# Where the high and low products of a row stand, and an even recurrence that is solved transposed, in a tuned four-layer trunk on one core

## The chip, the core and the metric

The kernel runs on one NeuronCore of a Trainium2 chip. Five engines run their own instruction streams and meet at semaphores: TensorE (PE, with its weight loads listed as PEld), VectorE (DVE), ScalarE (ACT), GpSimd (POOL) and SyncE (SP), which here issues all the DMAs. The metric is the device time of one execution in microseconds (us); lower is better.

## What is computed

Two layers over 256 tokens of width 2048 (fp32). Layer 0 is "even": one input projection feeds an RWKV-7 mixer (group A, 16 heads of 64) and an RG-LRU (group B), then one output projection. Layer 1 is "odd": sparse attention. Both are followed by a gated FFN of width 5632 and by a sigmoid-gated projection of p ("PLE").

```python
def reference(x, p, ...):
    for layer in range(DEPTH):
        j = layer // 2
        if layer % 2 == 0:
            z = x @ ev_w_in[j]
            y_a = rwkv7_mix(z[..., :A_COLS], ...)
            y_b = rglru_mix(z[..., A_COLS:], ...)
            y = jnp.concatenate([y_a, y_b], axis=-1) @ ev_w_out[j]
        else:
            y = dsa_mix(x, ...) @ od_w_out[j]
        x = layer_norm(DN_ALPHA * x + y, ln1_g[layer], ln1_b[layer])
        x = layer_norm(DN_ALPHA * x + conv_ffn(x, ffn_w_up[layer], ...), ln2_g[layer], ln2_b[layer])
        x = x + jax.nn.sigmoid(x @ ple_w_gate[layer]) * (p[layer] @ ple_w_proj[layer])

def rwkv7_mix(z, ...):
    ...
    def step(state, inp):
        r_t, w_t, k_t, v_t, kk_t, a_t = inp
        sa = jnp.einsum('bhvk,bhk->bhv', state, -kk_t)
        state = state * w_t[:, :, None, :] + sa[..., None] * (kk_t * a_t)[:, :, None, :] + v_t[..., None] * k_t[:, :, None, :]
        return state, jnp.einsum('bhvk,bhk->bhv', state, r_t)
    ...
    ym = jnp.mean(y, -1, keepdims=True)
    yv = jnp.mean(jnp.square(y - ym), -1, keepdims=True)
    y = ((y - ym) * lax.rsqrt(yv + A_GN_EPS)).reshape(bsz, seq, A_WIDTH) * gn_g + gn_b
    bonus = (jnp.sum(r * k * r_k, -1, keepdims=True) * v).reshape(bsz, seq, A_WIDTH)
    return ((y + bonus) * g).astype(z.dtype)
```

## The kernel before

Channels lie on partitions, the 256 tokens in the free dimension. Every large weight is read once, in chunks of 128x1024 (512 KB): `wchunk` (L143) has SP load it into `raw` (three buffers), ACT makes the rounded high half `hi`, DVE the rest `lo = raw - hi` (five buffers each). Activations x are split the same way, so that a product needs three parts: hi by x-high and x-low, lo by x-high.

**Rows of products.** In `mm3` (L164) a weight block of 128x128 is used in two matmuls, "H" (hi, 512 columns: both halves of x) and "L" (lo, 256 columns), or, with `one`, in three of 256 columns (L171 to L173). A row (one tile of 128 outputs) has 16 blocks, 44 in the FFN's down projection. The 88 rows of FFN up from row 3 on go through `ordered` (L178), in an order that `row_order(j)` (L41) gives: three rows of four are plain, H then L for each block (L then H in one group of five), and the last of four has in its second half a turn from HL to LH or back, eight H and then eight L ("8/8"), two H and then two L ("2/2", blocks 12 and 13), or one H split in two, each once in 20 rows. FFN down, the PLE gate, odout and evout are plain H, L.

**Even layer.** The 16 heads of A are done in 8 pairs i (128 channels, 4 chunks of 64 tokens). `stage1(i)` makes the pair's r, k, v from the input projection (`block`, three rows of 16 blocks with `one`) and the factors of the chunked recurrence (AR, be, ka, ...). `stage2(i)` solves the recurrence, as a chain that hops between PE, DVE and ACT: be by AR, whose diagonal 16x16 blocks are packed in `Y16`; X, which spreads Y16 over 128x512 twice; two matmuls of X by the constant `ones16` (L863) and two ACT copies, which put it as `B` on all partitions; 15 steps on DVE that invert the small blocks (`M`); their spread `Dt`; E by Dt (FT), Dt by RHS (Z1), three times FT by Z (`four`, L829: four fp32 matmuls of 128x128); gb by R1; then the four chunks in turn (L935 `ub` by R1, L936 `vb` by R2, L938 the state), and `cen` by y (L954), which takes the mean off y. fp32 products count two matmul records each in the trace. While a hop of stage2 is under way PE works on filler: `stage2` yields what it needs (table `W`, in us of filler), and `run` takes that from `filler(i)`: `stage1(i+1)`, then by `FILL` the RG-LRU block i (`rglru`, two rows of 16 blocks and two matmuls by `bw`); in the last pair rows of evout as well. Fillers use the `pp` banks of PSUM, the chain `a1` and `a2`. DVE and ACT work of the chain is put ahead of other work by `Ahead`.

**What sets the order.** Each engine runs its stream in a fixed order, laid out when the kernel is built; SP issues loads in stream order, and a load whose buffer or source isn't ready holds up those behind it.

## Time and profile before

| | |
|---|---|
| time, median of 3 runs | 2448.95 us (2446.68 to 2449.39) |
| the profiled execution's own time | 2452.36 us |
| its span | 2450.6 us |
| PE busy | 2418.4 us (99%) |
| DVE busy | 1789.5 us (73%) |
| ACT busy | 1396.4 us (57%) |
| DMA, mean | 175 GB/s |
| granted TensorE clock, mean | 0.998 |

The span is the time from the first to the last instruction of the profiled execution; its own time lies 1.8 us above. Busy is the sum over an engine's instructions; that of PE counts the modelled ends of pipelined matmuls, so it does not say that PE could not be faster. In the trace the even layer's pairs lie at about 0 to 400 us, evout to 507, FFN 0 at 507 to 1240, PLE 0 to 1356, the odd attention to 1503, odout to 1588, FFN 1 at 1600 to 2330, PLE 1 to 2441.

### The profile page before, as it was taken

The numbers are of one execution on the slowest core, as the hardware profiler recorded it, in microseconds if no ns is written. First come the engines' busy times: TensorE is split into PE (matmuls) and PEld (weight loads), VectorE is DVE, ScalarE is ACT, GpSimd is POOL, SyncE is SP. The second block draws the span as 40 slices with busy tenths as digits, with TensorE's granted clock in tenths as the row PEclk, the third lists the DMA queues.
The fourth block names the chain that finished last, engine by engine and source line by source line (L and its number), as shares of the span: only waits on it lengthen the run. The fifth ranks groups of instructions, "written<-read, shape, count | busy, mean of one in ns | idle before, by whom it ended". The sixth has DMA issues, their size and how long they took to land.

```text
span 2450.6 us, 40345 instructions
## 1 busy us (share of the span) xinstructions
PE 2418.4 (99%) x15144; PEld 2165.0 (88%) x15144; DVE 1789.5 (73%) x3580; ACT 1396.4 (57%) x2612; POOL 87.9 (4%) x98
## 2 busy tenths in 40 slices
...
GB/s 242 118 123 121 103 116 116 187 172 200 189 189 190 189 190 189 185 189 189 189 169 198 182 163 124 187 182 189 189 189 192 187 188 189 182 190 190 192 170 168
DMA packets 128484, 429.38 MB, mean 175 GB/s; under 512 B 14096, under 2 KB 21920, under 8 KB 128288
## 3 DMA queue, kind: packets, MB, share of 16 engines
...
q8 instruction: 119, 1.95, 0.3%
q14 instruction: 77, 0.63, 0.1%
...
## 4 chain that ended last, share of the span: by engine, by line
PE 92%; DVE 4%; ACT 3%; DMA 1%; issue 0%; POOL 0%; POOLq 0%; ACTq 0%; DVEq 0%
PE a L185 24%; PE pp L185 14%; PE a L175 11%; PE pp L175 11%; PE a L176 6%; PE pp L176 5%; PE pp L171 4%; PE pp L172 4%; PE pp L173 4%; PE a L829 2%; DVE lo L79 1%; PE a L171 1%; PE a L172 1%; PE a L173 1%; ACT hi L79 1%
## 5 line engine op out<-in xcount | busy, mean ns | idle before, releaser
L79 DVE TENSOR_TENSOR lo<-raw,hi 128x1024 fp32r<-128x1024 f32 (+4 forms) x1160 | 1007.8, 883 | 482.5 <-ACT hi L79 476.5
L79 ACT CAST hi<-raw 128x1024 fp32r<-128x1024 f32 (+4 forms) x1160 | 863.7, 770 | 729.9 <-PE a L185 146.1
L185 PE MATMUL a<-x,hi 128*128 128x512 f32 (+1 forms) x1718 | 593.1, 393 | 0.0
L185 PE MATMUL a<-x,lo 128*128 128x256 f32 x1712 | 468.8, 279 | 0.0
L185 PEld LDWEIGHTS a<-x,hi 128*128 128x128 f32 x1718 | 320.1, 187 | 72.2
L185 PE MATMUL pp<-x,hi 128*128 128x512 f32 x1010 | 352.0, 393 | 0.0
L185 PEld LDWEIGHTS a<-x,lo 128*128 128x128 f32 x1712 | 320.0, 188 | 1.8
L185 PE MATMUL pp<-x,lo 128*128 128x256 f32 x1008 | 278.2, 279 | 0.0
L175 PE MATMUL a<-g,hi 128*128 128x512 f32 x792 | 275.1, 391 | 0.0
L171 PE MATMUL pp<-x,hi 128*128 128x256 f32 x800 | 248.6, 311 | 6.6 <-ACT x L164 6.6
L172 PE MATMUL pp<-x,hi 128*128 128x256 f32 x800 | 227.3, 284 | 0.7 <-DVE x L165 0.7
L173 PE MATMUL pp<-x,lo 128*128 128x256 f32 x800 | 227.6, 284 | 0.0
L185 PEld LDWEIGHTS pp<-x,hi 128*128 128x128 f32 x1010 | 188.7, 187 | 42.9
L176 PE MATMUL a<-g,lo 128*128 128x256 f32 x792 | 221.8, 280 | 0.0
L372 DVE SCALAR_TENSOR_TENSOR cv<-u,vec_sb,cv 128x255 f32<-128x255 f32 x352 | 169.5, 482 | 56.1 <-ACT cv L369 50.1
L185 PEld LDWEIGHTS pp<-x,lo 128*128 128x128 f32 x1008 | 189.1, 188 | 0.6
L175 PE MATMUL pp<-g,hi 128*128 128x512 f32 x528 | 183.6, 391 | 0.0
L175 PEld LDWEIGHTS a<-g,hi 128*128 128x128 f32 x792 | 148.1, 187 | 32.5
L171 PEld LDWEIGHTS pp<-x,hi 128*128 128x128 f32 x800 | 154.1, 193 | 11.0 <-ACT x L164 6.6
L172 PEld LDWEIGHTS pp<-x,hi 128*128 128x128 f32 x800 | 154.2, 193 | 5.4 <-issue 3.6
L369 ACT ACTIVATE cv<-u,vec_sb 128x256 f32<-128x256 f32 x176 | 106.1, 603 | 85.4 <-DVE u L238 85.4
L173 PEld LDWEIGHTS pp<-x,lo 128*128 128x128 f32 x800 | 153.6, 192 | 0.2 <-issue 0.2
...
## 6 DMA issues: line engine op xcount, KB each, us to landing
raw<-up SPq DMA_DIRECT2D x352, 512.0 KB, 4.3
raw<-dn SPq DMA_DIRECT2D x160, 512.0 KB, 3.7
raw<-evin SPq DMA_DIRECT2D x86, 512.0 KB, 4.0
raw<-pg SPq DMA_DIRECT2D x64, 512.0 KB, 4.6
raw<-odout SPq DMA_DIRECT2D x32, 512.0 KB, 4.3
raw<-evout SPq DMA_DIRECT2D x16, 512.0 KB, 3.6
...
```

The lines of the kernel that those rows point to most:

```text
L79: return getattr(self.eng, name)(*args, **kw)
L171: nc.tensor.matmul(ps[:, 0:S], hi, hl[:, 0:S], start=first, stop=False)
L172: nc.tensor.matmul(ps[:, 0:S], hi, hl[:, S:2 * S], start=False, stop=False)
L173: nc.tensor.matmul(ps[:, 0:S], lo, hl[:, 0:S], start=False, stop=last)
L175: nc.tensor.matmul(ps[:, 0:2 * S], hi, hl, start=first, stop=False)
L176: nc.tensor.matmul(ps[:, 0:S], lo, hl[:, 0:S], start=False, stop=last)
L185: self.nc.tensor.matmul(out, w[:, c], x, start=(what, k) == order[0], stop=(what, k) == order[-1], skip_group_check=True)
L369: nc.scalar.activation(y, u, AF.Identity, bias=self.v(f"cb{l}", j), scale=self.v(f"cw2{l}", j))
L372: nc.vector.scalar_tensor_tensor(y[:, d:], u[:, 0:S - d], self.v(f"cw{n}{l}", j), y[:, d:], op0=ALU.mult, op1=ALU.add)
L829: T.matmul(ps[:, c * P:(c + 1) * P], lhs[:, c * P:(c + 1) * P], AR4[:, c] if rhs is AR else rhs[:, c * P:(c + 1) * P], start=True, stop=True)
```

## The change

**Orders of rows.** `row_order` goes. `dodge(j)` sets an order for two rows only: j = 0 has in its second half eight H then eight L, j = 1 has H H L L at blocks 12 and 13. FFN up calls it with (j - 3) modulo 29 (rows 3 and 4, 32 and 33, 61 and 62 of 88), the PLE gate with m - 3 (rows 3 and 4 of 16), odout with m (rows 0 and 1 of 16). All other rows are plain H, L.

**The even recurrence.** The product of be and what follows from it (Y16, ET, R1) move from stage2 to the end of stage1. B is no longer made by X, ones16 and two copies: Y16 is written to DRAM (`dd`, 128x64, one DMA) and read back eight times, each 4 KB onto 16 partitions of B. The system is solved transposed: M runs from 14 down to 0, ET by Dd gives HT, Dd by R1 gives Y1, three times HT by Y, each with an addition on DVE; then gb by Y, and the transposed ak by Y is added to R2, so that a chunk needs vb by R2 and the state, and no ub. v is centred as it is transposed (two fp32 matmuls by `cen` in the place of two transposes), and cen by y goes.

**The other group.** The eight RG-LRU blocks are one stream of filler, of which each of the pairs 0 to 6 takes 12.7 us by the planner's costs (`SHARE`), the last of these what is left; pair 7 has evout rows alone. `W` has other values. Further, stage1 takes twelve blocks of v (six before) ahead of the broadcast of the norms, the constant pool keeps its size (`PAD`), and the DMA scratch has another size.

```diff
+    def dodge(self, j):
+        self.order = None
+        if j in (0, 1):
+            o = [(c, k) for k in range(KD) for c in "HL"]
+            if j == 0:
+                o[16:] = [(c, k) for c in "HL" for k in range(8, KD)]
+            else:
+                o[24:28] = [(c, k) for c in "HL" for k in (12, 13)]
+            self.order = o
     def ordered(self, ps, hi, lo, hls, k0, order):

-        todo = [o for o in order if k0 <= o[1] < k0 + 8]
-        for what, k in todo:
+        for what, k in order[2 * k0:2 * k0 + 16]:
             c = slice((k - k0) * P, (k - k0 + 1) * P)
-            out, w, x = {"H": (ps[:, 0:2 * S], hi, hls[k]), "L": (ps[:, 0:S], lo, hls[k][:, 0:S]),
-                         "A": (ps[:, 0:S], hi, hls[k][:, 0:S]), "B": (ps[:, S:2 * S], hi, hls[k][:, S:2 * S])}[what]
+            out, w, x = (ps[:, 0:2 * S], hi, hls[k]) if what == "H" else (ps[:, 0:S], lo, hls[k][:, 0:S])
...
-                    self.order = row_order(j)
+                    self.dodge((j - FIRST) % DODGE)
...
+            self.dodge(m - FIRST)
...
-FILL = {0: [0], 1: [1], 2: [2], 3: [3], 4: [4], 5: [5], 6: [6], 7: [7]}
...
+SHARE = 12.7
+W = (1.0, 0.4, 1.8, 1.7, 1.9, 1.2, 0.5, 2.4, 2.8)
...
-        return AR, v, bp, kp, g, bo, PC
+        pb = q(self.four(bd["be"], lambda c: AR4[:, c]), 128)
+        yield 2 * F32_256
+        t = self.r1("dblk")
+        V.tensor_tensor(q(t), pb[:, :, 0:C], bc(k.c("maskD")[:, None, :], [P, NC, C]), op=ALU.mult)
+        Y16 = self.r1("y16")[:, 0:64]
+        V.tensor_reduce(Y16, t.rearrange("p (c b t) -> p c t b", b=4, t=16), axis=AX.X, op=ALU.add)
+        V.tensor_tensor(q(Y16, 16), q(Y16, 16), bc(k.c("id16")[:, None, :], [P, NC, 16]), op=ALU.add)
+        dd = self.dpool.tile([P, 64], F32, tag="dd", name=k.nm("dd"), bufs=2)
+        nc.sync.dma_start(dd, Y16)
+        B = self.newB()
+        ap = dd[:, :]
+        for b in range(8):
+            nc.sync.dma_start(B[b * 16:(b + 1) * 16, :], bass.AP(tensor=ap.tensor, offset=ap.offset + b * 1024, ap=[[0, 16], [1, 1024]]))
+        ET, R1 = (self.R.tile([P, 512], F32, tag=n, name=k.nm(n), bufs=1) for n in ("ET", "R1"))
+        V.tensor_tensor(q(R1, 128)[:, :, C:], pb[:, :, C:], bc(k.c("maskI")[:, None, :], [P, NC, C]), op=ALU.mult)
+        self.expand(ET, pb[:, :, 0:C], "maskE")
+        return AR, v, bp, kp, g, bo, PC, ET, R1, B
+    def four(self, lhs, rhs):
+        ps = self.a2()
+        for c in range(NC):
+            self.nc.tensor.matmul(ps[:, c * P:(c + 1) * P], lhs[:, c * P:(c + 1) * P], rhs(c), start=True, stop=True)
+        return ps
...
-        def tokmajor(src, dst, scale=None):
+        def tokmajor(src, dst, scale=None, by="ident", whole=False):

             ps = self.a2()
             for c in range(2):
-                T.transpose(ps[:, c * P:(c + 1) * P], src[:, c * P:(c + 1) * P], k.c("ident"))
+                cs = slice(c * P, (c + 1) * P)
+                if by == "ident":
+                    T.transpose(ps[:, cs], src[:, cs], k.c("ident"))
+                else:
+                    T.matmul(ps[:, cs], src[:, cs], k.c(by), start=True, stop=True)
...
-        pb = q(four(bd["be"], AR), 128)
...
-        Xs = []
-        for c2 in range(2):
-            X = self.r2("X")
-            V.tensor_tensor(X.rearrange("p (c t s) -> p c t s", t=16, s=16),
-                            bc(q(Y16, 16)[:, 2 * c2:2 * c2 + 2, :, None], [P, 2, 16, 16]),
-                            bc(k.c("id16")[:, None, None, :], [P, 2, 16, 16]), op=ALU.mult)
-            Xs.append(X)
-        ET, ak = self.r2("ET"), self.r2("ak")
...
+        ak, R2 = self.r2("ak"), self.r2("R2")
...
-        B = self.first.pop("B", None) or self.newB()
-        for c2, X in enumerate(Xs):
-            ps = self.a2()
-            T.matmul(ps, k.c("ones16"), X, start=True, stop=True)
-            A.copy(B[:, c2 * 512:(c2 + 1) * 512], ps)
-            yield W[2]
...
+        B4 = B.rearrange("p (s c t) -> p s c t", c=NC, t=16)
         Mt = self.t2("Mt")[:, 0:64]
         M3 = q(Mt, 16)
         V.tensor_copy(M3, bc(k.c("id16")[:, None, :], [P, NC, 16]))
-        for n in range(1, 16):
+        for n in range(14, -1, -1):
             tm = self.R.tile([P, 64], F32, tag="sub", name=k.nm("sub"), bufs=2)
-            tv = q(tm, 16)[:, :, 0:n + 1]
-            V.tensor_tensor(tv, B4[:, :, n, 0:n + 1], M3[:, :, 0:n + 1], op=ALU.mult)
+            tv = q(tm, 16)[:, :, n:]
+            V.tensor_tensor(tv, B4[:, n, :, n:], M3[:, :, n:], op=ALU.mult)
             V.tensor_reduce(M3[:, :, n], tv, axis=AX.X, op=ALU.add)
-            yield W[3]
-            if n == 2:
-                tokmajor(v, lambda h: vb4[:, :, h, :])
-            if n == 4:
+            yield W[1]
+            if n == 13:
+                tokmajor(AR[:, 0:S], lambda h: gb4[:, :, h, :], -1.0)
+            if n == 11:
+                tokmajor(bp, lambda h: q(R1, 128)[:, :, 0:C])
+            if n == 8:
                 ps = self.a2()
                 for c in range(NC):
-                    T.transpose(ps[:, c * P:(c + 1) * P], ET[:, c * P:(c + 1) * P], k.c("ident"))
-                E = self.r2("E")
-                A.copy(E, ps)
-            if n == 7:
-                ps = four(ak, bd["vb"])
-                p4 = ps.rearrange("p (c h f) -> p c h f", h=2, f=C)
-                self.halves(lambda h, s: A.copy(q(RHS, 128)[s, :, 0:C], p4[s, :, h, :]))
-            if n == 10:
-                tokmajor(bp, lambda h: q(R1, 128)[:, :, 0:C])
-            if n == 12:
+                    T.transpose(ps[:, c * P:(c + 1) * P], ak[:, c * P:(c + 1) * P], k.c("ident"))
+                akT = self.r2("akT")
+                A.copy(akT, ps)
+            if n == 5:
+                tokmajor(v, lambda h: vb4[:, :, h, :], by="cen")
+            if n == 2:
                 tokmajor(kp, lambda h: q(R2, 128)[:, :, 0:C])
-        Dt = self.r2("Dt")
-        V.tensor_tensor(Dt.rearrange("p (c b t) -> p c b t", b=8, t=16), bc(M3[:, :, None, :], [P, NC, 8, 16]),
+        Dd = self.r2("Dd")
...
+        ps = four(ET, Dd)
+        HT = self.r2("HT")
+        A.copy(HT, ps)
+        ps = four(Dd, R1)
+        Y1 = self.r2("Y1")
+        A.copy(Y1, ps)
+        Y = Y1
+        for n in range(3):
+            yield W[3]
+            ps = four(HT, Y)
+            Y = self.r2("Y")
+            V.tensor_tensor(Y, Y1, ps, op=ALU.add)
...
-        ps = four(E, Dt)
-        FT = self.r2("FT")
-        A.copy(FT, ps)
-        ps = four(Dt, RHS)
-        Z1 = self.r2("Z1")
-        A.copy(Z1, ps)
-        Z = Z1
-        for n in range(3):
-            yield W[5]
-            ps = four(FT, Z)
-            if n < 2:
-                Z = self.r2("Z")
-                V.tensor_tensor(Z, Z1, ps, op=ALU.add)
-        z4, p4 = Z1.rearrange("p (c x f) -> p c x f", x=2, f=C), ps.rearrange("p (c x f) -> p c x f", x=2, f=C)
-        for x, n in ((1, "gb"), (0, "ub")):
-            d4 = bd[n].rearrange("p (c h t) -> p c h t", h=2, t=C)
-            self.halves(lambda h, s: V.tensor_tensor(d4[s, :, h, :], z4[s, :, x, :], p4[s, :, x, :], op=ALU.add))
...
-        ps = four(bd["gb"], R1)
-        pv = q(ps, 128)
+        pv = q(four(bd["gb"], Y), 128)
...
+        ps = four(akT, Y)
+        V.tensor_tensor(R2, R2, ps, op=ALU.add)
...
-            T.matmul(ps[:, 0:P], bd["ub"][:, cs], R1[:, cs], start=True, stop=False)
-            T.matmul(ps[:, 0:P], bd["vb"][:, cs], R2[:, cs], start=False, stop=c == 0)
+            T.matmul(ps[:, 0:P], bd["vb"][:, cs], R2[:, cs], start=True, stop=c == 0)
...
-        ps = self.a2()
-        T.matmul(ps[:, 0:S], k.c("cen"), y, start=True, stop=True)
...
-        A.activation(sq, ps[:, 0:S], AF.Square, scale=0.125)
-        A.copy(yc, ps[:, 0:S])
+        A.activation(sq, y, AF.Square, scale=0.125)
...
-        for j in FILL.get(i, []):
-            yield from self.rglru(j, new(HP + j))
-        if i + 1 == HP:
+        if i + 1 < HP:
+            got = 0
+            while got < SHARE or i + 2 == HP:
+                t = next(self.others, None)
+                if t is None:
+                    break
+                got += t
+                yield t
+        else:

...
+                k.dodge(m)
```

Some places on the engines, in the instruction streams as they are laid out. PE, start of stage2 of the fourth pair before: X_2816 and X_2818 are the two halves of X, cst_sb the constant ones16, the rest blocks of filler.

```order
L172 MATMUL pp_2851<-x_119,hi_2853 128x256
L173 MATMUL pp_2851<-x_119,lo_2854 128x256
L863 MATMUL a_534_2890<-X_2816,cst_sb 128x512
L171 MATMUL pp_2851<-x_122,hi_2853 128x256
L172 MATMUL pp_2851<-x_122,hi_2853 128x256
L173 MATMUL pp_2851<-x_122,lo_2854 128x256
L863 MATMUL a_535_2899<-X_2818,cst_sb 128x512
```

PE after, at the place where stage2 of the fifth pair begins (AR_3267 by bd_ka):

```order
L312 MATMUL a_655_3591<-cst_sb,grb_3589 128x128 x2
L804 MATMUL a_659_3602<-AR_3267,bd_ka 128x128 x4
L702 MATMUL a_661_3611<-la,lora_2878 128x256
L709 MATMUL a_663_3617<-la,lora_2878 128x256
L143 MATMUL pp_3626<-x_96,hi_3628 128x256
L144 MATMUL pp_3626<-x_96,hi_3628 128x256
```

The products of X and be are not there any more; ka by AR is followed by the products of the next stage1.

PE before, hops of the same chain: FT by Z for the first and second time, with stage1's products (g, rk) between.

```order
L829 MATMUL a_589_3209<-Z_588_3195,FT_3188 128x128 x4
L767 MATMUL a_593_3220<-g_84,lora_2127 128x256
L768 MATMUL a_593_3220<-g_85,lora_2127 128x256
L774 MATMUL a_595_3226<-rk_3224,cst_sb 128x256
L829 MATMUL a_596_3228<-Z_3214,FT_3188 128x128 x4
```

PE after, the same hops as HT by Y, with AR_3267 by bd_be of the next pair behind them:

```order
L749 MATMUL a_584_3250<-g_86,lora_2167 128x256
L750 MATMUL a_584_3250<-g_87,lora_2167 128x256
L804 MATMUL a_585_3253<-Y_3218,HT_3174 128x128 x4
L756 MATMUL a_588_3263<-rk_3261,cst_sb 128x256
L804 MATMUL a_594_3284<-AR_3267,bd_be 128x128 x4
```

One product more, be of the next pair, stands in the gap that follows the second hop.

SP before, loads of the fourth and fifth pair's blocks (raw) and the lora weights:

```order
L153 DMA raw_3609<-evin 128x1024
L153 DMA raw_3674<-evin 128x1024
L651 DMA lora_3541<-lora 128x512
L153 DMA raw_3742<-evin 128x1024
L153 DMA raw_3801<-evin 128x1024
L153 DMA raw_3866<-evin 128x1024
```

SP after, at the place where the fifth pair's dd and B are issued:

```order
L125 DMA raw_3627<-evin 128x1024
L633 DMA lora_3609<-lora 128x512
L790 DMA dd_3294<-y_596_3291 128x64
L794 DMA B_3296<-dd_3294 16x1024 x8
L949 DMA bw_3562<-bw 128x256
L125 DMA raw_3684<-evin 128x1024
L125 DMA raw_3754<-evin 128x1024
L125 DMA raw_3815<-evin 128x1024
```

dd waits for Y16, and each of the eight parts of B for dd; the raw loads behind them wait in the stream.

## Rows read from the trace of the kernel before

**Rows 1.** The page: busy time of each engine (share of the span, instructions), and the chain of work that ended last, its shares by engine.

```profile
PE 2418.4 (99%) x15144; PEld 2165.0 (88%) x15144; DVE 1789.5 (73%) x3580; ACT 1396.4 (57%) x2612; POOL 87.9 (4%) x98
...
PE 92%; DVE 4%; ACT 3%; DMA 1%; issue 0%; POOL 0%; POOLq 0%; ACTq 0%; DVEq 0%
```

**Rows 2.** The busy time by stretch, here two pairs of four of the even layer (48.3 us each): window, its length, then for each engine busy us and instructions, granted clock, DMA share, GB/s; last the sum and mean over four pairs.

```profile
104.00:152.30 48.30, 48.15 (x382) 46.09 (x381) 40.84 (x137) 35.80 (x99) 2.35 (x2) 1.00 0.37 119
...
sum 193.20, PE 192.59 PEld 184.40 DVE 163.34 ACT 143.22 POOL 9.39; mean PE 48.15 PEld 46.10 DVE 40.84 ACT 35.80 POOL 2.35
```

**Rows 3.** The timeline of PE around the two products of X in the third pair: start, duration, engine, line, operation, tiles, shape, records. Between the rows left out only filler of the same kinds.

```profile
152.01 0.28 PE L173 MATMUL pp<-x,lo 128*128 128x256 f32 x1
...
152.37 1.10 PE L863 MATMUL a<-X,cst_sb 128*128 128x512 f32 x2
...
153.42 0.28 PE L172 MATMUL pp<-x,hi 128*128 128x256 f32 x1
...
153.54 0.28 PE L173 MATMUL pp<-x,lo 128*128 128x256 f32 x1
...
153.66 1.02 PE L863 MATMUL a<-X,cst_sb 128*128 128x512 f32 x2
...
154.63 0.28 PE L172 MATMUL pp<-x,hi 128*128 128x256 f32 x1
```

**Rows 4.** The same timeline at four other places of that pair: the transposes of v and the next filler; a hop of FT by Z; ub by R1 of a chunk and what follows; cen by y and what follows.

```profile
156.67 0.38 PE L814 MATMUL a<-cst_sb,v 128*128 128x128 f32 x2
...
157.01 0.28 PE L172 MATMUL pp<-x,hi 128*128 128x256 f32 x1
...
178.11 1.06 PE L829 MATMUL a<-Z,FT 128*128 128x128 f32 x8
...
179.12 0.28 PE L172 MATMUL pp<-x,hi 128*128 128x256 f32 x1
...
183.12 0.39 PE L935 MATMUL a<-R,bd_ub 128*128 128x128 f32 x2
...
183.35 0.39 PE L936 MATMUL a<-R,bd_vb 128*128 128x128 f32 x2
...
191.13 0.59 PE L954 MATMUL a<-y,cst_sb 128*128 128x256 f32 x2
...
191.56 0.59 PE L985 MATMUL a<-xc,bw 128*128 128x256 f32 x2
```

**Rows 5.** What PE waited for from 40 to 425 us: line, releaser, us in total, times, longest. These are the largest two rows.

```profile
PE a L829 <- ACT Z L79: 1.3, 2, 0.9
PE a L863 <- DVE R L79: 1.2, 1, 1.2
```

**Rows 6.** DVE in the four pairs of rows 2, by line, tile and shape: count, busy us, mean ns, idle before.

```profile
L79 DVE TENSOR_TENSOR Z<-Z,a 128x512 f32<-128x512 f32 x8 | 5.5, 687 | 0.5
L79 DVE TENSOR_TENSOR X<-y,cst_sb 128x512 f32<-128x512 f32 x8 | 5.2, 686 | 0.0
...
L79 DVE TENSOR_TENSOR bd_ub<-Z,a 64x256 f32<-64x256 f32 x8 | 3.3, 418 | 0.2
```

**Rows 7.** DMA issues: destination and source, queue, count, KB each, median us from issue to landing.

```profile
raw<-evin SPq DMA_DIRECT2D x86, 512.0 KB, 4.0
...
pp<-sp SPq DMA_DIRECT2D x16, 128.0 KB, 2.4
...
rb<-relb SPq DMA_DIRECT2D x1, 64.0 KB, 4.4
...
bias_tab<-tb SPq DMA_DIRECT2D x1, 24.0 KB, 1.5
```

**Rows 8.** What SP's queue waited for from 100 to 350 us: releaser, us in total, times, longest.

```profile
SPq L153 <- DVE lo L79: 204.8, 41, 13.3
```

**Rows 9.** The timeline of PE in FFN up of layer 0: after an 8/8 row, across the 2/2 row at 608 us, and after it. Rows left out are H and L products of the same kind.

```profile
587.14 0.40 PE L185 MATMUL a<-x,hi 128*128 128x512 f32 x1
...
607.64 0.40 PE L185 MATMUL a<-x,hi 128*128 128x512 f32 x1
...
607.99 0.63 PE L185 MATMUL a<-x,hi 128*128 128x512 f32 x2
608.46 0.39 PE L185 MATMUL a<-x,lo 128*128 128x256 f32 x2
608.69 0.40 PE L185 MATMUL a<-x,hi 128*128 128x512 f32 x1
...
628.45 0.39 PE L185 MATMUL a<-x,hi 128*128 128x512 f32 x1
```

**Rows 10.** Busy time in stretches of 19 us, columns as in rows 2: FFN up ahead of and behind the 2/2 row, FFN down, PLE 0, odout, PLE 1. The first bracket is the count of PE matmuls.

```profile
588.00:607.00 19.00, 19.00 (x110) 16.47 (x109) 13.26 (x21) 10.20 (x16) 0.00 (x0) 1.00 0.57 190
609.00:628.00 19.00, 19.00 (x112) 16.61 (x111) 13.71 (x21) 11.19 (x18) 0.00 (x0) 1.00 0.56 183
1030.00:1049.00 19.00, 19.00 (x112) 16.75 (x111) 9.37 (x12) 7.26 (x8) 0.00 (x0) 1.00 0.63 205
1300.00:1319.00 19.00, 19.00 (x109) 16.50 (x108) 17.05 (x31) 10.88 (x18) 0.00 (x0) 1.00 0.70 235
1520.00:1539.00 19.00, 19.00 (x109) 16.51 (x108) 14.50 (x25) 8.45 (x11) 0.00 (x0) 1.00 0.59 190
2400.00:2419.00 19.00, 19.00 (x109) 16.47 (x108) 15.81 (x26) 10.43 (x15) 0.00 (x0) 1.00 0.73 238
```

More of the change, by code (lines that the diff above doesn't have):

```diff
@@ L28 @@
 FIRST = 3
-PAD = 56
+DODGE = 29
+PAD = 184
 def drain(g):
@@ L38, in drain @@
             return e.value
-def row_order(j):
-    n = j // 4 % 5
-    pair = ["HL", "LH"]
-    last = j % 4 == 3
-    way = 1 if (n == 1) else 0
-    out = []
-    for k in range(KD):
-        if last and k >= 8:
-            if n == 0 and k >= 12:
-                out += [(c, k) for c in "LH"]
-                continue
-            if n == 1 and k >= 12:
-                out += [(c, k) for c in "HL"]
-                continue
-            if n == 2:
-                out += [("H", k)] if k < 15 else [("H", 15)] + [("L", i) for i in range(8, 16)]
-                continue
-            if n == 3 and k in (12, 13):
-                out += [] if k == 12 else [("H", 12), ("H", 13), ("L", 12), ("L", 13)]
-                continue
-            if n == 4 and k == 12:
-                out += [("A", 12), ("B", 12), ("L", 12)]
-                continue
-        out += [(c, k) for c in pair[way]]
-    return out
 class Ahead:
@@ L192, in gproj @@
         ps = self.ps()
-        order = self.order
-        self.order = None
+        order, self.order = self.order, None
         for k0 in range(0, KT, group):
@@ L491, in consts @@
     c["cen"] = eye - bd / 64
-    c["ones16"] = (p[:, None] // 16 == p[None, :] // 16)
     c["maskE"] = -(bd * (s[:, None] // 16 < s[None, :] // 16))
@@ L665, in setup @@
         self.bd = {}
-        for n in ("be", "ka", "vb", "ub", "gb"):
+        for n in ("be", "ka", "vb", "gb"):
             t = self.R.tile([P, 512], F32, name=f"bd_{n}")
@@ L749, in stage1 @@
         rest = block(2, v)
-        for _ in range(6):
+        for _ in range(12):
             yield next(rest)
@@ L796, in stage1, with expand @@
         V.tensor_tensor(q(bp), q(be), bc(PC, [P, NC, C]), op=ALU.mult)
-        return AR, v, bp, kp, g, bo, PC
+        pb = q(self.four(bd["be"], lambda c: AR4[:, c]), 128)
[20 more added lines that the diff above has]
+        return ps
+    def expand(self, out, src, mask):
+        V, mask = Ahead(self.k.tc, self.nc.vector, AHEAD1), self.k.c(mask)
+        V.tensor_tensor(out.rearrange("p (c h t) -> p c h t", h=2, t=C), bc(src[:, :, None, :], [P, NC, 2, C]),
+                        bc(mask.rearrange("p (h t) -> p h t", t=C)[:, None], [P, NC, 2, C]), op=ALU.mult)
     def stage2(self, i, state, yout):
@@ L826, in four @@
         def four(lhs, rhs):
-            ps = self.a2()
-            for c in range(NC):
-                T.matmul(ps[:, c * P:(c + 1) * P], lhs[:, c * P:(c + 1) * P],
-                         AR4[:, c] if rhs is AR else rhs[:, c * P:(c + 1) * P], start=True, stop=True)
-            return ps
-        def expand(out, src, mask):
-            V.tensor_tensor(out.rearrange("p (c h t) -> p c h t", h=2, t=C), bc(src[:, :, None, :], [P, NC, 2, C]),
-                            bc(mask.rearrange("p (h t) -> p h t", t=C)[:, None], [P, NC, 2, C]), op=ALU.mult)
@@ L850, in stage2 @@
-        ET, ak = self.r2("ET"), self.r2("ak")
-        RHS, R1, R2 = self.r2("RHS"), self.r2("R1"), self.r2("R2")
-        expand(ET, pb[:, :, 0:C], k.c("maskE"))
-        V.tensor_tensor(q(R1, 128)[:, :, C:], pb[:, :, C:], bc(k.c("maskI")[:, None, :], [P, NC, C]), op=ALU.mult)
-        pk = q(four(bd["ka"], AR), 128)
-        expand(ak, pk[:, :, 0:C], k.c("maskK"))
+            return self.four(lhs, lambda c: rhs[:, c * P:(c + 1) * P])
+        ak, R2 = self.r2("ak"), self.r2("R2")
+        pk = q(self.four(bd["ka"], lambda c: AR4[:, c]), 128)
@@ L866, in stage2 @@
-        B4 = B.rearrange("p (c t s) -> p c t s", t=16, s=16)
-        vb4 = bd["vb"].rearrange("p (c h t) -> p c h t", h=2, t=C)
+        gb4, vb4 = (bd[n].rearrange("p (c h t) -> p c h t", h=2, t=C) for n in ("gb", "vb"))
+        B4 = B.rearrange("p (s c t) -> p s c t", c=NC, t=16)
         Mt = self.t2("Mt")[:, 0:64]
@@ L943, in stage2 @@
             if c < NC - 1:
-                yield W[8]
+                yield W[6]
                 pt = self.a2()
@@ L1010, in rglru, with rglrus @@
         k.hl_split(yout, h)
+    def rglrus(self, new):
+        for j in range(HP):
+            yield from self.rglru(j, new(HP + j))
     def softplus(self):
```

31 lines of the change are left out of this document (11 added, 20 removed).

## The prediction

> **What bounds the kernel now.** The page comes first: PE is busy for 2418.4 of 2450.6 us, and of the chain that ended last 92% is PE [rows 1]. So the time is the sum of the spacings of PE's instructions, and an edit is worth what it takes out of PE's stream, less any wait that it puts there. Second, the stretches of the even layer show whether that holds where the recurrence runs: in each pair of 48.30 us PE is busy for 48.15, DVE for 40.84 and ACT for 35.80 [rows 2]. The chain of hops is hidden by filler. PE's list of waits agrees: from 40 to 425 us the two largest are 1.3 and 1.2 us in all [rows 5]. Third, since busy times of pipelined matmuls overlap, all prices are read from the timeline as distances between starts. A filler matmul of 256 columns takes 0.12 us (153.42 to 153.54 [rows 3]).
>
> **Removed from PE in each pair.** X by ones16 are two products of two records. From the first (152.37) to the L172 behind it (153.42) are 1.05 us, in which one L171 of 0.12 lies too: 0.93. The second: 153.66 to 154.63, less 0.12, is 0.85. From the L173 at 152.01 to 152.37 are 0.36, 0.24 more than a normal spacing [rows 3]. That is 1.78, with the lead-in 2.02; I take 1.9, since the same kind of lead-in may appear at another instruction. ub by R1: 183.12 to 183.35, 0.23, four times: 0.92 [rows 4]. cen by y: 191.13 to 191.56, 0.43 [rows 4]. Added: v's two transposes (156.67 to 157.01 less one filler, 0.22) become two fp32 matmuls of the kind of FT by Z, of which four take 178.11 to 179.12 less 0.12, 0.89 [rows 4], so 0.45 for two: +0.23. All other products keep their number and shape: E by Dt, Dt by RHS, three FT by Z, gb by R1 and ak by vb become ET by Dd, Dd by R1, three HT by Y, gb by Y and akT by Y; four transposes of ET become four of ak. Together -1.9 - 0.92 - 0.43 + 0.23 = -3.0 us a pair, eight pairs **-24 us** (bounds -23 and -25).
>
> **The shift of the RG-LRU blocks** removes nothing. A block is two rows of 16 blocks by three matmuls of 0.12, 11.5, and two products of 0.43: 12.4 us. Each of the first seven pairs gets a seventh more, 1.8, and so takes 48.3 - 3.0 + 1.8 = 47.1; the last loses the 12.4. It has only evout rows to cover its hops: 8 rows of 16 blocks by 0.353 (below), 45 us, and `W` asks for 25. Cost nothing; without that cover the last chain would stand open.
>
> **DVE** loses two X of 0.686 and four halves of 0.418, gains a third Y and the sum to R2, by the nearest row (Z, the same shape) 0.687 each [rows 6]: -1.7 a pair. A seventh of an RG-LRU block is added: its rows are two of the pair's five, so at most two fifths of 40.84, by seven: 2.3. DVE is then at 40.84 - 1.7 + 2.3 = 41.5 of 47.1 us, 88% for 85%. ACT loses copies. Neither becomes the bound by its sum. The order shows where the chain is tight: between the second and third HT by Y stand rk and be, 0.43 + 0.89 = 1.3 us of cover, in some pairs with filler behind. Before, FT by Z had g, g and rk there, three of 0.43, 1.3 too, and waited for Z 1.3 us in all [rows 5]. So nothing there, but be now stands in the gap, and be needs AR from DVE.
>
> **B by way of DRAM.** The trace has no such round trip. Nearest rows: 24 KB to DRAM 1.5 us and 128 KB back 2.4 for the write of 32 KB; for the read of 512 KB by eight transfers, 64 KB in 4.4 and a raw chunk of 512 KB in 4.0 [rows 7]. I take 2.4 + 4.4 = 6.8, with eight issues on SP some 9 us from Y16 to the last part of B. The Trainium skill ("DMA: Bandwidth & Descriptors", section on the anatomy of one DMA) gives a fit of about 2.0 us fixed plus the bytes by 436 GB/s: an estimate from it is 2.1 and 3.2, 5.3 us. By it the cover below would be 1.5 us more, and the sum the same. In the stream the products of stage1 and some 120 filler matmuls, 14 us, stand between be and ka by AR of pair five, and M begins behind ka. So from the third pair on the trip is hidden, with some 5 us to spare. The first two pairs have less: there the wait is between 0 and 3 us. Against it, the stalls of the first pair for X and Z [rows 5], 2.5 us, may go. I add **+1** (from -2 to +3).
>
> SP is the other place. dd waits for Y16, B for dd, and the raw loads behind for both. But SP is far ahead: of 250 us it waits 204.8 for a `lo` to set a buffer free [rows 8]. A chunk is 8 blocks by 0.36, 2.9 us of PE, and there are three raw buffers and five of hi and lo, so a load has up to 23 us until PE needs it. The loads behind dd are needed by PE a chunk or more behind ka, 14 + 2.9 = 17 us after be, and can be issued 9 us after be, to land 4.0 later. Cost nothing, with some 4 us of margin.
>
> **The orders of rows.** The timeline shows two spacings of the same H, L pairs at the same granted clock. After an 8/8 row: from 587.14 to 607.64 are 58 pairs, 0.3534 each. After the 2/2 row: from 608.69 to 628.45 are 57, 0.3467 each [rows 9]. The stretches agree: 110 matmuls in 19 us ahead of 2/2, 112 behind it, 112 in FFN down, whose rows are plain (1030), and 109 in PLE 0, odout and PLE 1 [rows 10]. So the spacing is a state that lasts: 2/2 leads to the fast one, plain rows keep either. Before, each 8/8 row of FFN up is followed by four slow rows, 61 pairs, until 2/2, four times a layer: 4 x 61 x 0.0067 = 1.6 us. After, three times 12 pairs are slow between row j = 0 and j = 1: 0.24. FFN 0 gains 1.4, FFN 1 1.8 (before, one more slow stretch of 20 us). odout is fast from its second row on: 13 full rows of 16 pairs by 0.0067, 1.4. PLE has ten rows behind its 2/2: 1.1 each, 2.2. Sum **-6.5** (bounds 0 and -7). I hold it likely since 2/2 follows 8/8 by 12 pairs in the change and by 60 before, both multiples of three, and the slow timeline repeats every three pairs.
>
> The first two terms and the +1 give -29.5 against the profiled execution's 2452.4, 2423; the median of the runs is 3.4 lower: **2420 us**.
>
> **Rivals.** (a) *New waits take half of the even gain.* For: DVE at 88%, be in the third hop's gap, the chain shorter on PE while DVE's part is as long. Against: the waits of before, 3 us over 385, at a cover as thin. Price: 1.5 us a pair, 12 us: 2432. It decides if PE waits for DVE or B in most pairs. (b) *Slower: SP's stream stops at dd.* If Y16 comes later than SP's lead allows, each pair stops PE for the round trip of 6.8 us: eight pairs, +54, less the gains of 30: 2473. For: eight transfers of one source wait in line with the loads of weights. Against: the margin of 4 us above; it decides from 4 us of lateness. (c) *The rows keep the slow spacing.* If 2/2 doesn't lead to the fast state any more, FFN up and down (2 x 2064 pairs, now some 3600 of them fast) all run at 0.3534: +24 in place of -6.5, so 2450. For: nothing explains the state. Against: it recurs at all eight 2/2 rows. (d) *The order does nothing.* The timeline shows 0.3467 and 0.3534 for the same pair [rows 9]; if that difference hangs on something else in these stretches, -6.5 falls away: 2426. [...]
>
> **How the numbers follow.** The forecast has 62%, (a) 17%, (d) 9%, (c) 7%, (b) 5%. The likeliest case spans 2413 to 2427 by its bounds (even -25, -7, -2 to even -23, -4, +3). The range takes in (a) and (d): 2412 to 2436. A measurement can tell about 0.2%, 5 us. Faster: the forecast, (a) and (d), less 1% for mishaps: 87%. Same: most of (c), 5%. Slower: (b) and the rest, 8%.
>
> **What would show it.** In the changed trace: pairs of 47.1 us in the even layer with PE's waits below 3 us in all; no ones16 product; dd to landing 1.5 to 2.4 and the last part of B 4 to 5 us after its issue, with no PE wait for M or Dd behind the second pair; 112 matmuls in 19 us in odout and PLE from the sixth row on, as in FFN; evout as before. Wrong would be: PE waiting on DVE for Y or R2, raw loads landing after their use, or 109 to 110 matmuls per 19 us in FFN down.

## The result and the profile after

The changed kernel takes **2436.55 us** (median of 5 runs, 2435.01 to 2438.87), the kernel before 2449.34 beside it: 0.995 of it, 95% interval 0.9935 to 0.9964. That is 12.8 us less, where 29 were forecast, and 0.55 us above the range. The profiled execution's span is 2437.1 us (its own time, 2438.87, is the longest of the five, and the profiled execution before, 2452.36, lies 3 us above its median too: differences between traces are good to a few us). The page after, to be held against [rows 1]:

```profile
PE 2392.0 (98%) x15040; PEld 2142.1 (88%) x15040; DVE 1779.5 (73%) x3548; ACT 1376.3 (56%) x2574; POOL 86.8 (4%) x97
...
PE 88%; DVE 5%; ACT 4%; DMA 2%; issue 1%; POOL 0%; DVEq 0%; ACTq 0%; POOLq 0%
```

PE has lost 26.4 us of busy time, about what the forecast took off. But the span has lost 13.5, and the chain that ended last is PE for 88% of its length, 92% before. The start of the first sum of the layer norm that follows evout divides the span: PE reached it at 507.43 us before, and after at

```profile
501.47 0.42 PE L272 MATMUL a<-cst_sb,acc 128*128 128x32 f32 x3
```

so the even layer gave 6.0 us (23 forecast), and all that follows 7.5 (6.5 forecast). The even layer in stretches of 48 us (columns as in [rows 2]; the second, and the sum and mean of four):

```profile
148.00:196.00 48.00, 45.81 (x367) 45.19 (x366) 39.95 (x132) 33.59 (x91) 2.30 (x2) 0.96 0.41 127
...
sum 192.00, PE 181.96 PEld 177.55 DVE 161.38 ACT 138.74 POOL 9.01; mean PE 45.49 PEld 44.39 DVE 40.34 ACT 34.69 POOL 2.25
```

Before, PE was busy for 48.15 of 48.30 us; now for 45.49 of 48 on the mean, while DVE and ACT are no fuller. The second stretch has a mean granted clock of 0.96 (a dip from 2.4 to 1.2 GHz, below). The largest of PE's waits from 40 to 425 us (compare [rows 5]):

```profile
PE a L321 <- ACT sq L51: 6.4, 5, 2.2
PE a L804 <- ACT Y L51: 3.3, 4, 1.4
PE a L804 <- DVE Dd L51: 2.1, 2, 1.4
PE a L804 <- ACT bd_be L51: 1.3, 1, 1.3
```

All rows of that view add up to 17.1 us, 2.9 before. L321 sums the squares of kk in stage1, L804 are the hops of the chain. The rows of products behave as forecast (compare [rows 10]: FFN up, PLE 0, odout, PLE 1):

```profile
600.00:619.00 19.00, 19.00 (x112) 16.61 (x111) 13.67 (x22) 11.09 (x17) 0.00 (x0) 1.00 0.61 191
1290.00:1309.00 19.00, 19.00 (x112) 16.60 (x111) 18.16 (x33) 11.03 (x19) 0.00 (x0) 1.00 0.66 204
1520.00:1539.00 19.00, 19.00 (x112) 16.59 (x111) 14.43 (x25) 8.52 (x10) 0.00 (x0) 1.00 0.63 191
2390.00:2409.00 19.00, 19.00 (x111) 16.63 (x110) 16.07 (x26) 10.31 (x16) 0.00 (x0) 1.00 0.74 237
```

112 matmuls in 19 us, the fast spacing, now also in PLE 0 and odout, which had 109; 111 in PLE 1.

### The profile page after: what moved, and what is told of

It is laid out like the page before. It is cut to its first block, busy times and chain, and to the rows that moved or that the text cites. A ratio compares the mean times of both kernels' runs of the same rounds, so it can differ in the third digit from the quotient of the medians.

```text
span 2437.1 us, 40155 instructions
## 1 busy us (share of the span) xinstructions
PE 2392.0 (98%) x15040; PEld 2142.1 (88%) x15040; DVE 1779.5 (73%) x3548; ACT 1376.3 (56%) x2574; POOL 86.8 (4%) x97
## 4 chain that ended last, share of the span: by engine, by line
PE 88%; DVE 5%; ACT 4%; DMA 2%; issue 1%; POOL 0%; DVEq 0%; ACTq 0%; POOLq 0%
PE a L147 26%; PE pp L147 18%; PE a L148 13%; PE pp L148 9%; PE pp L144 3%; PE pp L143 3%; PE pp L145 3%; PE a L167 2%; PE a L804 2%; PE pp L167 2%; DVE lo L51 2%; DMA raw<-evin 1%; ACT hi L51 1%; PE a L143 1%; PE a L144 1%; PE a L145 1%
## 5 line engine op out<-in xcount | busy, mean ns | idle before, releaser
L147 PE MATMUL a<-x,hi 128*128 128x512 f32 x1904 | 670.7, 395 | 8.8 <-DVE x L301 8.8
L148 PE MATMUL a<-x,lo 128*128 128x256 f32 x1904 | 529.3, 278 | 0.0
L147 PEld LDWEIGHTS a<-x,hi 128*128 128x128 f32 x1904 | 358.5, 188 | 93.6 <-DVE x L301 10.5
L147 PE MATMUL pp<-x,hi 128*128 128x512 f32 x1136 | 402.6, 396 | 3.5 <-DVE x L301 3.4
L148 PEld LDWEIGHTS a<-x,lo 128*128 128x128 f32 x1904 | 359.0, 189 | 0.4 <-DVE lo L51 0.2
L148 PE MATMUL pp<-x,lo 128*128 128x256 f32 x1136 | 315.5, 278 | 0.0
L147 PEld LDWEIGHTS pp<-x,hi 128*128 128x128 f32 x1136 | 213.7, 188 | 55.8 <-DVE x L301 6.1
L143 PE MATMUL pp<-x,hi 128*128 128x256 f32 x800 | 239.8, 300 | 7.4 <-ACT x L136 6.5
L145 PE MATMUL pp<-x,lo 128*128 128x256 f32 x800 | 229.2, 287 | 1.0 <-DVE lo L51 1.0
L144 PE MATMUL pp<-x,hi 128*128 128x256 f32 x800 | 229.3, 287 | 0.7 <-DVE x L137 0.7
L148 PEld LDWEIGHTS pp<-x,lo 128*128 128x128 f32 x1136 | 214.0, 188 | 0.1
L143 PEld LDWEIGHTS pp<-x,hi 128*128 128x128 f32 x800 | 154.7, 193 | 8.1 <-ACT x L136 6.5
L144 PEld LDWEIGHTS pp<-x,hi 128*128 128x128 f32 x800 | 154.8, 193 | 1.7 <-DVE x L137 1.2
L145 PEld LDWEIGHTS pp<-x,lo 128*128 128x128 f32 x800 | 154.5, 193 | 1.5 <-DVE lo L51 1.4
```

The lines of the kernel that those rows point to most:

```text
L143: nc.tensor.matmul(ps[:, 0:S], hi, hl[:, 0:S], start=first, stop=False)
L144: nc.tensor.matmul(ps[:, 0:S], hi, hl[:, S:2 * S], start=False, stop=False)
L145: nc.tensor.matmul(ps[:, 0:S], lo, hl[:, 0:S], start=False, stop=last)
L147: nc.tensor.matmul(ps[:, 0:2 * S], hi, hl, start=first, stop=False)
L148: nc.tensor.matmul(ps[:, 0:S], lo, hl[:, 0:S], start=False, stop=last)
```

## Two places where PE waits

**A late load.** PE, a hop of the fifth pair; ACT at the same time; and the longest of the ten loads in the chain that ended last (three before):

```profile
271.33 1.05 PE L804 MATMUL a<-Dd,ET 128*128 128x128 f32 x8
272.22 1.06 PE L804 MATMUL a<-R,Dd 128*128 128x128 f32 x8
...
276.78 0.94 PE L804 MATMUL a<-Y,HT 128*128 128x128 f32 x6 [1.35 <-ACT Y L51]
```

```profile
273.81 1.64 ACT L51 CAST hi<-raw 128x256 fp32r<-128x256 f32 x5 [2.12 <-DMA raw<-evin]
275.35 0.58 ACT L51 COPY HT<-a 128x512 f32<-128x512 f32 x1
...
276.14 0.59 ACT L51 COPY Y<-a 128x512 f32<-128x512 f32 x1
```

```profile
266.93 6.86 DMA raw<-evin
```

PE has ET by Dd and Dd by R1 done by 273.3 us and could go on with HT by Y. ACT, which has to copy HT and Y for it, stands for 2.12 us at the cast of a chunk that was issued at 266.93 and took 6.86 us to land. The two copies are behind that cast in ACT's stream. PE waits 1.35 us.

This load did not itself wait for dd: the fifth pair's last part of B was issued at 239.81. What held it was a buffer. From 240 to 262 us, SP's longest wait and ACT's casts of the first chunk behind the trip:

```profile
SPq L125 <- DVE sub L51: 14.6, 1, 14.6
```

```profile
253.56 0.40 ACT L51 CAST hi<-raw 128x256 fp32r<-128x256 f32 x1
...
258.70 1.02 ACT L51 CAST hi<-raw 128x256 fp32r<-128x256 f32 x3
```

That chunk was issued at 240.80 and had landed by 246.0. ACT waited for other work in between and reached the casts only at 253.56 and 258.70, where they stand in its stream. The next load could go out at 260.50, when the buffer was free, and those up to 266.93 followed closely. With GpSimd's issue (b_on_pool, below) the same chunk was issued at 231.55 and its first cast began at 236.06. So in this pair the trip seems to act first through the place of the casts in ACT's stream, and only then through a late landing.

**A full ACT.** PE at the fourth pair's squares of kk, while the third pair's chain runs, and ACT ahead of it:

```profile
166.40 0.63 PE L321 MATMUL a<-cst_sb,sq 128*128 128x32 f32 x4 [2.19 <-ACT sq L51]
```

```profile
157.86 1.11 ACT L51 ACTIVATE bd_gb<-a 64x128 f32<-64x128 f32 x4
158.99 1.08 ACT L51 COPY R<-a 64x128 f32<-64x128 f32 x4
...
160.41 1.62 ACT L51 CAST hi<-raw 128x256 fp32r<-128x256 f32 x5
162.05 0.59 ACT L51 COPY akT<-a 128x512 f32<-128x512 f32 x1
162.53 0.48 ACT L669 ACTIVATE kr<-pp,omu 128x256 f32<-128x256 f32 x1
162.90 1.02 ACT L51 CAST hi<-raw 128x256 fp32r<-128x256 f32 x3
164.13 0.51 ACT L51 ACTIVATE kk<-kr,vec_sb 128x256 f32<-128x256 f32 x1 [0.21 <-DVE kr L670]
164.54 0.39 ACT L51 CAST hi<-raw 128x256 fp32r<-128x256 f32 x1
164.84 1.07 ACT L51 COPY bd_vb<-a 64x128 f32<-64x128 f32 x4
165.93 0.42 ACT L51 ACTIVATE sq<-kk 128x256 f32<-128x256 f32 x1
```

From 157.86 on ACT has no gap but 0.21 us: copies of three groups of transposes (bd_gb, R, bd_vb, four each), akT and nine casts lie around kr and kk, and sq comes at 165.93. PE waits 2.19 us and the granted clock then is at half for 3.4 us. No load is late here. In the kernel before the groups of copies lay further apart: the first four, RHS, bd_vb, E (at 159.88) and R, took 13 us where these four take 8:

```profile
152.89 1.13 ACT L79 ACTIVATE RHS<-a 64x128 f32<-64x128 f32 x4
...
157.46 1.10 ACT L79 COPY bd_vb<-a 64x128 f32<-64x128 f32 x4
...
164.83 1.08 ACT L79 COPY R<-a 64x128 f32<-64x128 f32 x4 [0.53 <-PE a L814]
```

## Experiments

The experiments ran in three groups, each beside the kernel before (2448.1 to 2448.9 us); the first two rows are from the group of the result. "Even" is the time of the layer norm's first sum as above, "waits" the sum of PE's from 40 to 425 us; both are read from one traced execution of each kernel.

| kernel | us | ratio, 95% interval | even | waits |
|---|---|---|---|---|
| before | 2449.34 | 1 | 507.4 | 2.9 |
| changed | 2436.55 | 0.995 (0.9935 to 0.9964) | 501.5 | 17.1 |
| rows_only | 2443.68 | 0.9983 (0.9974 to 0.9992) | 507.0 | 2.9 |
| b_on_pool | 2429.61 | 0.9926 (0.9911 to 0.994) | 490.7 | 9.7 |
| norm_later | 2439.22 | 0.9964 (0.9951 to 0.9977) | 505.4 | 17.8 |
| one_block_a_pair | 2445.66 | 0.9989 (0.9979 to 0.9999) | 509.3 | 23.1 |
| trip_sync | 2458.02 | 1.0038 (1.0026 to 1.0049) | 516.1 | 10.3 |
| trip_gpsimd | 2447.29 | 0.9992 (0.9982 to 1.0002) | 504.4 | 1.7 |
| b_by_ones | 2450.49 | 1.0005 (0.9996 to 1.0014) | 511.5 | 13.8 |
| pool_late_transposes | 2426.36 | 0.9907 (0.9893 to 0.9922) | 489.3 | 7.9 |
| share_only | 2449.15 | 1.0004 (0.9995 to 1.0014) | 508.4 | 4.8 |
| pool_one_block | 2438.15 | 0.9962 (0.9947 to 0.9977) | 504.9 | 17.2 |
| pool_norm_later | 2429.34 | 0.9917 (0.9902 to 0.9932) | 491.1 | 9.5 |
| pool_late_cover | 2428.35 | 0.9919 (0.9904 to 0.9933) | 489.8 | 8.9 |

Two theories at the outset: *loads* (the trip of B holds SP's stream, the raw chunks behind it come late) and *crowding* (the transposed chain's own copies fill ACT and DVE where stage1 needs them).

**rows_only**: the kernel before, with `dodge` in the place of `row_order`.

> The kernel before with the new orders of rows alone, the even recurrence as it was. Theory A (the orders give 6.5 us as forecast, and 18 of the 24 us of the even layer are lost to new waits): 2442 to 2443 us, and FFN 0 up to the end of down 1.4 us shorter. Theory B (the orders give most of the 12.8 us of the whole change): 2437 to 2439. If the orders give nothing: 2449.

The even layer keeps its 507, what follows is 7.9 us shorter in the trace, and the time 4.4 us (interval 2.0 to 6.4). So theory A: the loss is in the even layer. The orders give 4.4 us; the 6.5 forecast lie just outside the interval, and the time 0.7 us above theory A's range.

The order is not the whole of the state, though. trip_sync (below) has the old orders, and its odout runs at the fast spacing; pool_late_cover has the new ones, and its odout runs at the slow one:

```profile
1520.00:1539.00 19.00, 19.00 (x112) 16.60 (x111) 15.15 (x27) 8.51 (x10) 0.00 (x0) 1.00 0.63 202
```

```profile
1505.00:1524.00 19.00, 19.00 (x109) 16.51 (x108) 14.14 (x24) 8.51 (x11) 0.00 (x0) 1.00 0.58 185
```

Of four traces with the old orders, both PLE and odout are slow in two (before, trip_gpsimd) and fast in two (trip_sync, share_only). What else sets the state is not shown.

**b_on_pool**:

```diff
-        nc.sync.dma_start(dd, Y16)
+        nc.gpsimd.dma_start(dd, Y16)
...
-            nc.sync.dma_start(B[b * 16:(b + 1) * 16, :], ...)
+            nc.gpsimd.dma_start(B[b * 16:(b + 1) * 16, :], ...)
```

> The changed kernel, with the nine DMAs of dd and B issued by GpSimd instead of SyncE, so that no weight load stands behind them. Loads theory (SP is held at dd and B, raw chunks land late, ACT stands in order at a cast, and the copies of HT and Y behind it are late): ACT's waits for raw fall from 14 us to under 3, PE's for Y and Dd from 6 to under 2, time 2428 to 2432. Crowding theory: 2435 to 2438, ACT's waits for raw as before. If GpSimd's issue is slow, B comes later and PE waits for Dd more: over 2440.

The waits of PE and ACT with GpSimd's issue, then the layer norm's start:

```profile
PE a L321 <- ACT sq L51: 3.6, 4, 1.6
PE a L804 <- DVE Dd L51: 2.0, 2, 1.4
```

```profile
ACT hi L51 <- DMA raw<-evin: 4.5, 3, 2.1
```

```profile
490.65 0.42 PE L272 MATMUL a<-cst_sb,acc 128*128 128x32 f32 x3
```

With SyncE's issue ACT waited for

```profile
ACT hi L51 <- DMA raw<-evin: 14.1, 12, 2.5
```

so its waits for raw fall from 14.1 to 4.5 us (under 3 expected), PE's for Y go, the even layer is 10.8 us shorter in the traces, and the time 6.9. So most of the even layer's loss goes with the trip's place in SP's stream; sq (3.6) and Dd (2.0) stay. How it acts is shown less well, since the edit changes more than the issue: the build lays the streams out anew, and up to 430 us only 672 of ACT's 815 instructions stand in the same order in both traces. Nor are ACT's waits for raw a price by themselves. In pool_one_block (below), with GpSimd's issue, they are larger than in the changed kernel:

```profile
ACT hi L51 <- DMA raw<-evin: 27.7, 13, 4.8
```

What SP waited for from 48 to 425 us in the changed kernel, and how long its DMAs took:

```profile
SPq L790 <- DVE y L51: 27.3, 6, 6.6
...
SPq L794 <- DMA dd<-y: 11.4, 6, 2.7
```

```profile
raw<-evin SPq DMA_DIRECT2D x67, 512.0 KB, 3.8
B<-dd SPq DMA_DIRECT2D x64, 64.0 KB, 2.3
...
dd<-y SPq DMA_DIRECT2D x8, 32.0 KB, 1.9
```

dd waits 27.3 us in all for Y16 to be made (L790) and B 11.4 for dd to land (L794), with the weight loads behind. From the k-th raw load to the k-th chunk's first use by PE (100 to 370 us) it was never under 22.8 us before; in the changed kernel the least is 9.0, with GpSimd 20.3.

**trip_sync, trip_gpsimd**: the kernel before, with the nine DMAs added right behind Y16, into a tile that nothing reads, and the changed kernel's DRAM pool and size of the DMA scratch; the products stay as they were. The diff is that of trip_sync; trip_gpsimd has `nc.gpsimd` in it.

```diff
+        dd = self.dpool.tile([P, 64], F32, tag="dd", name=k.nm("dd"), bufs=2)
+        nc.sync.dma_start(dd, Y16)
+        B2 = self.R.tile([P, 1024], F32, tag="B2", name=k.nm("B2"), bufs=1)
+        ap = dd[:, :]
+        for b in range(8):
+            nc.sync.dma_start(B2[b * 16:(b + 1) * 16, :], bass.AP(...))
```

> The kernel before, plus the trip of Y16 to DRAM and back (the same nine DMAs by SyncE) into a tile that nothing reads; its own X, ones16 and copies still make B. Loads theory (SP, held at dd and B, lets raw chunks come late): PE's waits from 48 to 445 us rise from 3.7 to between 8 and 15 us, and the time to 2453 to 2462. Crowding theory (the transposed chain's own ACT and DVE order is the cause): no change, 2448.

> The kernel before plus the same unread trip, with its nine DMAs issued by GpSimd. Loads theory: no weight load stands behind them, so 2448 to 2450, 4 to 12 us below the run with SyncE. If the trip costs by its traffic (512 KB more a pair) and not by its place in SP's stream: the same as with SyncE.

PE's waits and SP's with SyncE, then PE's with GpSimd:

```profile
PE a L829 <- ACT Z L79: 6.6, 8, 1.0
```

```profile
SPq L844 <- DVE y L79: 38.1, 7, 5.6
SPq L848 <- DMA dd<-y: 13.4, 8, 3.7
```

```profile
PE a L869 <- DVE R L79: 1.1, 1, 1.1
```

9 us are lost with SyncE, none with GpSimd, and the even layer differs by 11.7. The bytes moved are the same, so the loss comes with the issue from SP's stream and not with the traffic. One thing was not expected: ACT does not stand at a cast here, and no load is short for PE (least lead 24.2 us). The two builds have PE's stream alike but for a few rows, while ACT's and DVE's differ: with SyncE the casts are laid out later and lie in front of FT and Z. So the trip in SP's stream can cost in two ways, by loads that land late and by where the build then puts the casts; here it seems to be the second alone. These runs don't separate the two shares in the changed kernel.

**b_by_ones**: the changed kernel with X, `ones16` and two copies again, no trip (`PAD` smaller to make room for the constant, and filler asked for behind each copy).

> The changed kernel with B made by X, ones16 on PE and two ACT copies again, in stage1, and no trip. Loads theory: PE's waits as in the run with GpSimd (about 9 us) or less, but 1.9 us of products in each pair come back, 15 us: 2442 to 2446, above the changed kernel. If waits from the trip cost as much as the products, 2436. Crowding theory: 17 us of waits stay and 15 come back: 2450 or more, as B adds two copies to ACT.

```profile
PE a L321 <- ACT sq L51: 11.1, 7, 2.9
```

2450.5 misses what the loads theory gave (2442 to 2446) and is what the crowding theory gave (2450 or more), though its waits are 13.8 us and not 17. Against b_on_pool the even layer is 20.8 us longer: 15 for the products, and 4.1 more waits, all that remain of size at sq. B's two copies and X's two DVE operations are put into stage1, where kk and sq are made. So there is crowding too, without any trip in SP's stream.

**norm_later, pool_norm_later**: `for _ in range(14)` in the place of 8 ahead of `group_pow`, with SyncE's and with GpSimd's issue.

> The changed kernel, with the product that sums the squares of kk (PE waits for ACT's sq there, 6.5 us in five places) put 14 blocks instead of 8 behind the row of kr. Crowding theory (ACT is full with the copies of the bunched transposes when kk and sq come, and only that place is short): these waits go, and the clock dip behind one of them, 7 to 9 us: 2428 to 2430. If what is late stays late and PE only waits at the next hop (the broadcast of the norms): 2435 to 2438.

> The changed kernel with GpSimd's issue of the trip, and the squares of kk summed 14 blocks behind the row of kr instead of 8. If the waits for sq that are left (3.6 us, with the refill of PE's pipeline some 4.5) are a matter of that place alone: 2424 to 2426. If the delay moves to the next hop, as it did with SyncE's issue: 2429 to 2433.

The waits at sq fall (6.4 to 1.5 us with SyncE's issue, 3.6 to none with GpSimd's), and others rise: 17.8 and 9.5 in all, as without the edit, and no time is won. That is the second answer of both expectations, with 2439.2 us 1 us above its range. But the delay did not go to the broadcast of the norms, as they had it: with GpSimd's issue it is at Dd (3.0 for 2.0) and at two products of the first pair (1.9 and 1.1).

**pool_late_transposes**: b_on_pool with two of the five groups of transposes at the hops.

```diff
-            if n == 13:
-                tokmajor(AR[:, 0:S], lambda h: gb4[:, :, h, :], -1.0)
...
-            if n == 2:
-                tokmajor(kp, lambda h: q(R2, 128)[:, :, 0:C])
...
             ps = four(HT, Y)
+            if n == 0:
+                tokmajor(AR[:, 0:S], lambda h: gb4[:, :, h, :], -1.0)
+            if n == 1:
+                tokmajor(kp, lambda h: q(R2, 128)[:, :, 0:C])
```

> The changed kernel with GpSimd's issue of the trip, and two of the five groups of transposes (AR and kp, each with four ACT copies of 0.27 us) moved from the M loop to the hops behind Y1, away from stage1's kk and sq. Crowding theory for what is left: PE's waits for sq (3.6 us with GpSimd's issue) fall below 1 us, and 2424 to 2427. If they are no cause: 2429 to 2430; if the copies are late for their new hop: above 2431.

```profile
PE a L804 <- DVE Dd L51: 2.1, 3, 0.9
PE a L804 <- DVE Y L51: 1.6, 2, 1.4
...
PE a L321 <- ACT sq L51: 1.2, 1, 1.2
```

sq falls to one wait of 1.2 us and the time to 2426.36, the best of all: 10 us below the changed kernel, 0.9907 of the kernel before. Taking copies away from sq takes its waits away, where moving sq only shifted them. What that is worth is less sure: 3.2 us against b_on_pool by the medians of four runs each, with intervals that overlap, and in the traces only 1.3 us of it lie in the even layer.

**pool_late_cover**: the same with `W[2]` 3.0 for 1.8 and `W[3]` 2.2 for 1.7.

> The run with GpSimd's issue and the later transposes, with 1.2 us more filler asked for ahead of Dd by ET and 0.5 us more at each hop of HT by Y. PE's waits for Dd and Y there were 2.1 and 1.6 us. If cover is what they lack: 2422 to 2425. If the cause is DVE's or ACT's order, which moves along: 2426 to 2428.

The broadcast of the norms now waits 3.2 us for DVE, 8.9 in all, and the time is 2428.35: no gain, 0.4 us above the second answer. More cover at one hop moved the wait to another.

**share_only, one_block_a_pair, pool_one_block**: the spread of the RG-LRU blocks added to the kernel before, and taken from the changed one (SyncE, GpSimd).

```diff
-            got = 0
-            while got < SHARE or i + 2 == HP:
...
+            yield from self.rglru(i, new(HP + i))
+        if i + 1 == HP:
+            yield from self.rglru(i, new(HP + i))
```

> The kernel before with its RG-LRU blocks spread over seven pairs (SHARE) and nothing else. As forecast for this part (it removes nothing and the cover is enough): 2447 to 2450. If the spread is worth what the changed kernel loses without it (9 us): 2439 to 2442. If the last pair, without a block, stands open: 2452 to 2458.

> The changed kernel, with one RG-LRU block in each of the eight pairs as before, instead of spread over seven. If the spread makes the new waits (a block then begins and ends at another place in each pair, and its ACT and DVE work meets other parts of the chain): PE's waits from 40 to 425 us fall from 17 to under 6 us, 2424 to 2427. If the waits come from the transposed chain itself: 2434 to 2439.

> The changed kernel with GpSimd's issue of the trip and one RG-LRU block a pair. If the 9 us that the changed kernel loses without the spread come from SP's stream (the loads of a block stand behind dd and B at another place): 2428 to 2431. If the transposed chain needs the longer pairs as cover on ACT and DVE: 2436 to 2440.

On the kernel before the spread gives nothing (1.0004). Without it the changed kernel loses 9.1 us, and with GpSimd's issue 8.5, so it is not SP's stream. PE's largest wait in pool_one_block:

```profile
PE a L804 <- ACT bd_be L51: 8.0, 4, 3.0
```

be, which now ends stage1, waits 8.0 us in four places for ACT's copies of bd_be (1.3 us in one place with the spread). one_block_a_pair's 2445.66 lies above both answers of its expectation: the spread does not make the waits, it takes some away.

## Why the prediction was wrong, point by point

- **The products removed, -24 us: right.** With GpSimd's issue the even layer is 16.8 us shorter than before at 6.8 us more waits: 23.6 without them, and some 1 us more if the emptying of PE's pipeline at each wait is counted (below).
- **The orders of rows, -6.5: right in kind, too large in size.** The traces show 7.5 and 7.9 us after the even layer, but the trace before is a long execution; by the medians the orders gave 4.4 us (2.0 to 6.4). The terms of the sum add up to 6.8, not 6.5. Rival (c) falls: FFN keeps the fast spacing. Rival (d) falls in part: the orders do move the state in rows_only, yet trip_sync and share_only reach the fast spacing in PLE and odout with the old orders. The prediction had the slow spacing of these stages from one trace.
- **B's trip: hidden, as said.** dd took 1.9 us and each part of B 2.3 to land, less than the 2.4 and 4.4 taken; M began 15 to 19 us behind dd's issue, 7 to 12 us behind the landing of the last part of B. The Trainium skill ("DMA: Bandwidth & Descriptors", section on the anatomy of one DMA) gives its 2.0 us fixed plus bytes by 436 GB/s for DMAs that GpSimd issues; by it dd's 32 KB take 2.1 us, an estimate. dd took 1.9 issued by SyncE, and 2.7 issued by GpSimd in b_on_pool, 1.8 in trip_gpsimd; no run here has one transfer of 512 KB from dd.
- **SP, "cost nothing, with some 4 us of margin": the step that failed.** It reckoned from the moment when PE needs a chunk. But ACT casts it first, in order: from a raw load's issue to its cast there were 8.0 us in the middle and 4.1 at the least before, with landing in 4.0 [rows 7]. That stage had next to no margin in places, and what stands behind a cast on ACT is the chain's own copies. It also took the streams of ACT and DVE as given, while the build lays them out around the held loads. Price: 6.9 us by the medians (10.8 in the traces) between the two issues of the changed kernel. The signs of being wrong that the prediction named watched PE's use of a load, which was never late (9.0 us of lead at the least), and not ACT's cast. Rival (b) named the place and the mechanism, but priced it as a stop of PE for the whole trip (+54) and made it unlikely.
- **DVE and ACT, "neither becomes the bound by its sum": true and beside the point; the second step that failed.** The sums hardly moved; the copies of ACT moved together in front of sq. Rival (a) was right in kind, 12 us of price for 14.2 of waits, and wrong in where: it named DVE and the third hop, which wait 0.4 us in the whole trace. It was ACT, at sq, and the first hop.
- **+1 for the first pairs:** be of the first pair waits 1.3 us, Dd and Y there 1.8 more, none of it for B.
- **The shift of blocks, nothing:** right for the old chain, wrong for the new one, which needs it (9 us).
- **The likeliest case, "2413 to 2427 by its bounds":** the bounds it names give 2415 to 2425 from 2449.

The even layer's account: -24 forecast for the products, +14.2 of waits, +1.7 for the 3.4 us at half clock, and 2.2 for PE's pipeline, which empties at each wait, give -5.9; measured -6.0 in the traces. The 2.2 are an estimate: 18 waits against 4, and a filler matmul lasts 0.28 us at a spacing of 0.12, so some 0.16 each.

So 6.9 of the 16.6 us between forecast and result go with SP's issue and some 3 with the two moved groups of copies; the best kernel is still 6 us above 2420. Open: the shares of late landing and of the casts' place in ACT's stream, what sets the spacing of the rows besides their order, and the 8 us of waits that are left in the best kernel.
